# When a planned load that reuses a stored buffer counts as ready: landing instead of queue order

## The chip, the cores and the metric

The kernel runs on one core of one Trainium2 chip. The metric is the device time of one execution in microseconds (us); less is better. In the profile the engines are PE (TensorE), PEld (its weight loads), DVE (VectorE), ACT (ScalarE), POOL (GpSimd) and SP (SyncE). Here SP only issues DMA transfers, nearly all of them.

## What is computed

One layer of a streaming encoder in fp32 for 512 prompt tokens and 64 sample tokens, 576 in all, with D = 1024:

```python
mod = silu(c) @ w_ada + b_ada                    # six shift/scale/gate vectors of 1024
h = rms_normalize(x) * g_norm_mix * (1 + sc1) + sh1
q, k, v, qi, ki, wi, z, xbc, dt, gates = split(h @ w_in)
o_attn = dsa_attention(...)                      # indexer, top-k keys per query, softmax
y = ssd_scan(conv(xbc), dt, ...)                 # chunked scan, 8 groups; gated by silu(z), group norm
mixed = (sig(g1) * (o_attn @ w_branch_attn) + sig(g2) * (y @ w_branch_ssm)) @ w_out
x = x + gt1 * mixed
h2 = rms_normalize(x) * g_norm_ffn * (1 + sc2) + sh2
gate, up = split(h2 @ w_gate_up)                 # DFF = 2816
x = x + gt2 * ((silu(gate) * up) @ w_down)
```

It returns the new x, the new k, v and indexer keys, and the conv and scan states.

## The kernel before, in words

**Arithmetic.** Activations stand feature by token: 128 features on the partitions, and the 576 tokens as two halves of 288 (TH). Every fp32 operand is split into a rounded high part and the rest (wh and wl for weights, mh and ml, yh and yl and so on for activations), and a product is three matmuls: high by high, high by low, low by high. An output tile of 128 features, both halves, over 1024 inputs is 48 matmuls of 288 columns. A weight tile is loaded by SP into `raw` (two buffers), copied by ACT into `wh`, and subtracted by DVE into `wl`.

**Stages.** Modulation and norm at the start; w_in with the indexer, attention and 32 filler tiles (gates and z); conv and scan by groups g = 0 to 7; the branch projections; the output projection w_out with residual (`residual`, line 1681); the feed-forward, whose first two feature tiles are 16 plain products (twelve matmuls each) and the others seven products each of a Strassen scheme; w_down.

**The planner.** Nothing in the order of the instructions is written out by hand. `build` records every operation in a `Plan`. `_touch` (line 296) finds dependencies from the boxes of tiles that an operation reads and writes: `raw` (read after write), `waw`, and `war`, the latter also from the first writer of a buffer to all users of the tile that had the buffer before. A box is a bounding interval, on chip by partition and byte column, in a scratch tensor by offset. Two pieces with a stride, whose intervals interleave, thus count as overlapping even where they share no element.

`order` (line 402) then runs a list schedule over five engines with its own cost table (`cost`, line 347; `LATENCY`, line 233). `enable` is called for an operation once all its predecessors are placed; it works out the time t from which it is ready. Of the engine that is free first, the operation that is ready and has the smallest priority number (its place in the program, moved by `R.prio`) is placed. What the rules for t say is all the planner knows of waiting. For a DMA on SP, placed at time `at`, it reckons

```python
queue = max(at, queue) + 0.46
dma_free = max(queue + 1.3, dma_free) + op.xfer
op.t1 = dma_free + op.dur_dma
```

where t1 is the landing, `dur_dma` is 0.93, and `op.xfer` is the larger of bytes at `rate` (300e3 bytes per us after the start) and runs * (11.5 + 0.0358 * run bytes) / 16e3; SP itself is free again at once, or 2 us before `dma_free`. `emit` (line 573 issues everything, which is why each row of the profile has that line) hands the list to the tile framework in the planned order. Each engine executes its list in that order. The framework adds the semaphore waits that the buffers need, those of a load on the landing of an earlier store from the same buffer among them, whatever the planner assumed.

**Around the output projection.** `x2` are the tiles of the residual stream, tag `x2` with four buffers in pool `x1p`: `load_x2(a)` (line 1641) loads tile a from the scratch tensor x_d; `residual(a, ps, hf, last)` adds the projected tile to it, and behind the second half stores it and refills the buffer:

```python
if hf == 1:
    sync.dma_start(x2_d[:, a], x2[a])
    if 4 <= a + 3 < 8:
        load_x2(a + 3)
```

So `load_x2(4)` takes the buffer of x2[0], and so on to 7. The profile leaves buffer numbers out of names: both x_d and x2_d are `x_d` there, x2 is `x`, `x_d<-x` is the store of x2, `x<-x_d` the refill, and `x_d<-xs` the six stores of the input near the start (`store_x`, line 938).

In the same stage `ada_columns(7, ffw, 2, ("T3", "T4"), ("T1", "T2"))` (line 1699) works out one part of the modulation on DVE: eight pieces of w_ada of 256 KB go through the two tags T1 and T2, two buffers each (`T<-in_w_ada`), are multiplied and summed into T3 and T4, which sixteen small matmuls with `pick` bring together (`px<-T,pick`). `load_f(f)` (line 1784) loads the gate and up columns of feature tile f, tags `raw` and `rawu`, two buffers each; `prepare` (line 1802) splits them, for f = 1 partly into the tag `wx`. The last three tiles of w_out (a = 5, 6, 7) are done half by half, with accumulators in `mm` (two buffers, shared with the whole kernel) and `px`.

**Other places where a transfer follows a transfer in the same buffer.** `key_stack` (line 1157) loads a cache block twice into interleaved columns of one tile (`kisd`, `kd`, `kstd`). The narrow tile of w_in is loaded in two parts into one `raw`. The tiles g of the attention branch (four buffers) are loaded, gated, stored to m_d, and their buffers loaded again. The scratch tensors x_d, z_d, o_d, m_d and x2_d are written piece by piece with strides.

Of the kernel before, what the change touches and what calls it, by code (L numbers as in the profile page):

```python
# [229 lines left out]
class Plan:  # L230
# [171 lines left out]
    def order(self):  # L402
# [19 lines left out]
        def enable(op):  # L422
            closed = [p for p in op.pools if not p.open]
            if closed:
                held.setdefault(closed[0], []).append(op)
                return
            t = max((x[0].wait[x] for x in op.spots if x[0].kw.get("space") is None), default=0.0)
            for d, kind in op.deps.items():
                q = ops[d]
                if kind == "order" or q.mm and op.mm:  # L430
                    t = max(t, q.t0)
                elif kind == "raw" or q.eng != op.eng:
                    t = max(t, q.t1 + self.LATENCY[q.eng][op.eng] + op.slack)
            op.since = t
            heapq.heappush(future[op.eng], (t, op.prio, op.i))
# [25 lines left out]
        def fire():  # L461
            nonlocal now_ev
            while now_ev < len(self.events):
                what, p = self.events[now_ev]
                if what == "close" and p.ops_left:
                    return
                if p.kw.get("space") is None:
                    (place if what == "open" else leave)(p)
                seq.append((what, p))
                now_ev += 1  # L470
                if what == "open":
                    p.open = True
                    for op in held.pop(p, []):
                        enable(op)

        fire()
        for op in ops:
            if op.left == 0:
                enable(op)
        n = 0  # L480
        while n < len(ops):
# [16 lines left out]
            op = ops[i]  # L498
            if best == "tensor":
                if at - op.since < HOLD and self.change(form, op.form) > 0.1:  # L500
                    same = [x for x in r if ops[x[1]].form == form]
                    if same:
# [4 lines left out]
                        op = ops[x[1]]  # L507
                at += self.change(form, op.form)
                form = op.form
            if op.port:  # L510
                if port > at and best == "vector":
                    held_back = [(pr, i)]
                    while r and op.port and len(held_back) < 6:
                        pr, i = heapq.heappop(r)
                        held_back.append((pr, i))
                        op = ops[i]
                    pr, i = held_back.pop() if not op.port else held_back.pop(0)
                    op = ops[i]
# [22 lines left out]
            for s in op.succ:  # L541
                ops[s].left -= 1
                if ops[s].left == 0:
                    enable(ops[s])
# [1457 lines left out]
```

## Time and profile before

| | us |
|---|---|
| median of 3 runs | 1383.86 |
| lowest and highest | 1383.17 and 1384.22 |
| the profiled execution | 1383.03 |
| its span, first to last instruction | 1381.1 |
| busy in it: PE, DVE, ACT, POOL | 1356.7, 1071.9, 724.3, 209.8 |
| DMA, 190.19 MB, mean rate | 138 GB/s |

The profiled execution takes 1.9 us beyond its span. A busy PE isn't PE at its peak, since matmuls are pipelined and their ends modelled; what counts here are the gaps between them and the clock that was granted, which is 0.998 of full speed over the whole span. SP's rows are the instructions that issue transfers; their landing shows in the rows of what waits for them, and in the table of issues with the median time to landing.

### The profile page before, as it was taken

To read this page: it belongs to the slowest core of one execution; us is meant where nothing else is said; L and a number is where in the kernel's file an instruction comes from. 1 tells how busy PE (TensorE), PEld (TensorE's weight loads), DVE (VectorE), ACT (ScalarE), POOL (GpSimd) and SP (SyncE) were. 2 spreads that over 40 slices of the span, in tenths; PEclk is the share of its full clock that TensorE was granted. 3 is DMA by queue.
4 is the path that set the end of the run, shared out by engine and by line. 5 is a ranking of instruction groups with operands and counts; after the bars stand their busy time and mean duration, and the time that the engine had idled before them with its cause. 6 is when DMAs were issued, how large, how long until landed. Compare 5 with 4: busy or idle time off the path is not lost.

```text
span 1381.1 us, 27476 instructions
## 1 busy us (share of the span) xinstructions
PE 1356.7 (98%) x10731; PEld 1318.6 (95%) x10731; DVE 1071.9 (78%) x2115; ACT 724.3 (52%) x1542; POOL 209.8 (15%) x297
## 2 busy tenths in 40 slices
PE   7999999999999999999999999998999999999998
PEld 5999999999999999999999999998999999999998
DVE  5579997887878679888887688877899888887421
ACT  5444333767776655666665341224676666671221
POOL 2111003320300134444333300000000000000000
PEclk9999999999999999999999999999999999999999
DMA  9552347462753544344446477756233333326430
GB/s 324 164 132 83 113 121 205 115 164 69 194 135 88 129 120 118 110 125 133 121 118 189 135 217 228 251 180 205 72 92 93 92 94 103 95 87 215 141 110 29
DMA packets 252145, 190.19 MB, mean 138 GB/s; under 512 B 24768, under 2 KB 222640, under 8 KB 252016
## 3 DMA queue, kind: packets, MB, share of 16 engines
q1 hardware_dynamic: 248864, 177.87, 43.6%
q0 software_dynamic: 3104, 10.55, 4.1%
q8 instruction: 84, 1.38, 0.4%
q14 instruction: 45, 0.37, 0.1%
q10 hardware_dynamic: 48, 0.02, 0.0%
HBM read 153.09 MB, written 24.83 MB: 129 GB/s over the span
## 4 chain that ended last, share of the span: by engine, by line
PE 83%; DVE 9%; ACT 4%; DMA 2%; issue 1%; POOL 0%; SPq 0%; DVEq 0%; ACTq 0%; POOLq 0%
PE mm L573 61%; PE py L573 13%; PE px L573 9%; DVE cu L573 2%; DVE score L573 1%; DVE wl L573 1%; DVE m L573 1%; ACT wh L573 1%; DMA x_d<-x 1%; DMA T<-in_w_ada 1%; ACT dec L573 1%; DVE xb L573 1%; DMA rawu<-in_w_gate_up 0%; DMA rowsS<-in_c_sample 0%; DMA bc<-acs_d 0%
## 5 line engine op out<-in xcount | busy, mean ns | idle before, releaser
L573 ACT ACTIVATE wh<-raw 128x1024 fp32r<-128x1024 f32 (+1 forms) x159 | 156.4, 986 | 240.5 <-PE mm L573 193.1
L573 PE MATMUL mm<-hTl,wh 128*128 128x288 f32 x1152 | 262.5, 303 | 0.0
L573 PE MATMUL mm<-hTh,wl 128*128 128x288 f32 x1152 | 262.4, 303 | 0.0
L573 PE MATMUL mm<-hTh,wh 128*128 128x288 f32 x1152 | 259.9, 303 | 1.8 <-ACT hTh L573 1.8
L573 DVE TENSOR_TENSOR wl<-raw,wh 128x1024 fp32r<-128x1024 f32 (+1 forms) x117 | 142.2, 1217 | 86.4 <-ACT wh L573 81.8
L573 PEld LDWEIGHTS mm<-hTh,wl 128*128 128x128 f32 x1152 | 188.2, 189 | 2.8 <-issue 0.7
L573 PEld LDWEIGHTS mm<-hTh,wh 128*128 128x128 f32 x1152 | 186.2, 189 | 3.7 <-ACT hTh L573 2.1
L573 PEld LDWEIGHTS mm<-hTl,wh 128*128 128x128 f32 x1152 | 187.9, 189 | 1.6
L573 DVE SCALAR_TENSOR_TENSOR cu<-xc,wc,cu 128x579 f32<-128x579 f32 x96 | 90.3, 940 | 5.1 <-ACT cu L573 3.9
L573 PE MATMUL mm<-xhS,wh 128*128 128x290 f32 (+1 forms) x376 | 83.5, 296 | 0.0
L573 PE MATMUL mm<-xhS,wl 128*128 128x288 f32 (+1 forms) x360 | 80.0, 296 | 0.0
L573 DVE SCALAR_TENSOR_TENSOR aacc<-adr,sil,aacc 128x512 f32<-128x512 f32 x98 | 68.1, 744 | 6.6 <-DMA adr<-in_w_ada 6.6
L573 PE MATMUL mm<-wl,hTh 128*128 128x256 f32 x256 | 72.3, 284 | 0.1
L573 PE MATMUL mm<-wh,hTl 128*128 128x256 f32 x256 | 72.1, 284 | 0.0
L573 PE MATMUL mm<-wh,hTh 128*128 128x256 f32 x256 | 71.7, 283 | 0.0
L573 PE MATMUL mm<-xlS,wh 128*128 128x288 f32 (+1 forms) x252 | 65.9, 297 | 0.0
L573 PEld LDWEIGHTS mm<-xhS,wh 128*128 128x128 f32 x376 | 62.6, 188 | 0.0
L573 PEld LDWEIGHTS mm<-xhS,wl 128*128 128x128 f32 x360 | 60.0, 189 | 0.0
L573 PE MATMUL mm<-yl,wh 128*128 128x288 f32 x256 | 55.5, 297 | 0.0
L573 PE MATMUL mm<-yh,wl 128*128 128x288 f32 x256 | 55.0, 296 | 0.0
L573 PE MATMUL mm<-yh,wh 128*128 128x288 f32 x256 | 54.8, 296 | 0.0
L573 ACT ACTIVATE P<-lg,mn 128x128 f32<-128x128 f32 (+4 forms) x72 | 41.8, 581 | 24.8 <-DVE mn L573 23.9
(462 smaller groups left out, 3596.8 us busy)
## 6 DMA issues: line engine op xcount, KB each, us to landing
raw<-in_w_in SPq DMA_DIRECT2D x80, 512.0 KB, 4.0
adr<-in_w_ada SPq DMA_DIRECT2D x44, 512.0 KB, 5.7
rawu<-in_w_gate_up SPq DMA_DIRECT2D x22, 512.0 KB, 3.9
raw<-in_w_gate_up SPq DMA_DIRECT2D x22, 512.0 KB, 3.8
wl<-raw POOLq DMA_DIRECT2D x20, 512.0 KB, 4.8
bc<-acs_d SPq DMA_DIRECT2D x32, 256.0 KB, 3.4
raw<-in_w_branch_ssm SPq DMA_DIRECT2D x16, 512.0 KB, 4.6
raw<-in_w_down SPq DMA_DIRECT2D x16, 512.0 KB, 4.3
```

Source lines behind the costliest of these rows:

```text
L573: getattr(engines[x.eng], x.fn)(*[real(a) for a in x.args], **{k: real(v) for k, v in x.kw.items()})
```

## The change

One condition in `enable`, in the loop over the predecessors `d` of an operation (`q` is the predecessor, t1 its end and for a transfer its landing, t0 its start):

```diff
                 if kind == "order" or q.mm and op.mm:
                     t = max(t, q.t0)
-                elif kind == "raw" or q.eng != op.eng:
+                elif kind == "raw" or q.eng != op.eng or q.fn == "dma_start":
                     t = max(t, q.t1 + self.LATENCY[q.eng][op.eng] + op.slack)
```

Before, a `war` or `waw` predecessor on the operation's own engine put no bound on t. After, it puts t behind the landing, where that predecessor is a transfer. No operation, buffer, priority or cost is changed. What changes is the list that the planner makes, from the first place on where such a pair alters a choice.

## The prediction

> **What bounds the kernel now.** I read the page first, for the engine that sets the time.
>
> ```profile
> PE 1356.7 (98%) x10731; PEld 1318.6 (95%) x10731; DVE 1071.9 (78%) x2115; ACT 724.3 (52%) x1542; POOL 209.8 (15%) x297
> ```
>
> TensorE is busy in all but 1381.1 - 1356.7 = 24.4 us of the span. The change adds and removes no instruction; it only reorders queues. So it can win no more than part of those 24.4 us, and what counts is where they lie. The table of stretches says (after the stretch: its length, then busy time of PE, PEld, DVE, ACT and POOL; then granted clock, DMA share, GB/s):
>
> ```profile
> 800.00:920.00 120.00, 120.00 (x945) 118.19 (x944) 101.22 (x157) 33.49 (x48) 0.44 (x4) 1.00 0.72 224
> 920.00:960.00 40.00, 36.25 (x284) 34.74 (x283) 29.61 (x62) 17.72 (x40) 0.50 (x2) 0.98 0.66 200
> 960.00:1000.00 40.00, 39.96 (x297) 39.73 (x296) 30.02 (x57) 21.95 (x47) 2.01 (x4) 0.98 0.33 101
> 1000.00:1230.00 230.00, 230.00 (x1717) 229.84 (x1716) 203.11 (x356) 154.28 (x301) 0.00 (x0) 1.00 0.31 90
> ```
>
> Between 800 and 1230 us TensorE stops only in one place, 920:960, where the output projection hands over to the feed-forward part. It loses 3.75 us there. The timeline of TensorE shows the gaps (in brackets, idle before and what ended it):
>
> ```profile
> 952.72 0.29 PE L573 MATMUL px<-mh,wh 128*128 128x288 f32 x1
> 953.85 0.43 PE L573 MATMUL px<-T,pick 128*32 128x128 f32 x8 [0.85 <-DVE T L573]
> 954.52 0.43 PE L573 MATMUL px<-T,pick 128*32 128x128 f32 x8 [0.24 <-DVE T L573]
> ...
> 956.59 0.40 PE L573 MATMUL px<-mh,wl 128*128 128x288 f32 x1 [1.32 <-DVE wl L573]
> ...
> 958.47 0.61 PE L573 MATMUL mm<-mh,wh 128*128 128x288 f32 x1 [1.35 <-DVE x L573]
> ```
>
> 0.85 + 0.24 + 1.32 + 1.35 = 3.76 us, each time VectorE being late. The chain of waits says why VectorE is late (start, duration, what):
>
> ```profile
> 942.30 6.90 DMA x_d<-x
> ...
> 950.16 5.75 DMA rawu<-in_w_gate_up
> ```
>
> The path runs through the landing of a store of x2 (the profile drops buffer numbers: here x is a tile x2, x_d is x2_d), and then through a weight load queued behind it. SyncE's waits have the sum (us, times, longest), and its timeline the places:
>
> ```profile
> SPq L573 <- DMA x_d<-x: 15.6, 4, 5.4
> ```
>
> ```profile
> 925.13 0.34 SPq L573 DMA_DIRECT2D x_d<-x  x1
> ...
> 927.32 0.33 SPq L573 DMA_DIRECT2D x<-x_d  x1
> ...
> 933.43 0.33 SPq L573 DMA_DIRECT2D x_d<-x  x1
> 939.00 0.33 SPq L573 DMA_DIRECT2D x<-x_d  x1
> 939.44 1.66 SPq L573 DMA_DIRECT2D T<-in_w_ada  x2
> ...
> 942.30 2.55 SPq L573 DMA_DIRECT2D x_d<-x  x1
> 949.25 0.34 SPq L573 DMA_DIRECT2D x<-x_d  x1
> 949.64 0.42 SPq L573 DMA_DIRECT2D T<-in_w_ada  x1
> 950.16 0.38 SPq L573 DMA_DIRECT2D rawu<-in_w_gate_up  x1
> 950.63 0.53 SPq L573 DMA_DIRECT2D x_d<-x  x1
> 956.65 0.33 SPq L573 DMA_DIRECT2D x<-x_d  x1
> ```
>
> Four times a store of x2 is followed by the load that refills its buffer; SyncE stands at the load until the store has landed (from issue to the next load: 2.2, 5.6, 6.95 and 6.0 us), and the loads of T and rawu stand behind it. The planner of before believes such a load is ready at once, because store and load share a queue.
>
> **The change part by part.** The planner now holds a same-queue successor of a transfer until the transfer's modelled landing. For a store of x2 (294,912 B in runs of 2,304 B) its own formulas give 0.46 + 1.30 + 0.98 + 0.93 + 0.10 = 3.77 us. That is no time of the chip, only the length of the hold. During it SyncE takes other ready transfers. By the buffer rules these pairs are hit:
>
> (a) *The four refills of x2.* The third is worth the most. SyncE finished issuing the store at 942.30 + 2.55 = 944.85; T and rawu, now at 949.64 and 950.16, can go out at about 944.9 and 945.4, 4.7 us earlier. What they release:
>
> ```profile
> 953.05 1.42 DVE L573 SCALAR_TENSOR_TENSOR T<-T,sil,T 128x512 f32<-128x512 f32 x2 [3.64 <-DMA T<-in_w_ada]
> 954.38 1.03 DVE L573 SCALAR_TENSOR_TENSOR x<-mm,gt1h,x 128x256 f32<-128x256 f32 x3
> 955.32 1.22 DVE L573 TENSOR_TENSOR wl<-raw,wh 128x1024 fp32r<-128x1024 f32 x1
> 956.59 1.29 DVE L573 TENSOR_TENSOR wx<-rawu,wx 128x512 fp32r<-128x512 f32 x2
> ...
> 966.10 0.64 DVE L573 SCALAR_TENSOR_TENSOR x<-px,gt1h,x 128x256 f32<-128x256 f32 x2 [0.92 <-PE px L573]
> ```
>
> ```profile
> 955.93 1.15 ACT L573 ACTIVATE wx<-rawu 128x512 fp32r<-128x512 f32 x2 [5.42 <-DMA rawu<-in_w_gate_up]
> ```
>
> VectorE was free 3.64 us before 953.05, so its pair on T starts at 949.4; wl, right behind, ends at 956.54 - 3.64 = 952.9. TensorE, which leaves its last unhindered matmul at 952.85, then meets T and wl on time: 0.85, 0.24 and 1.32 us go. The last wait hangs on rawu: landing at 955.91 - 4.7 = 951.2, ScalarE then splits it, VectorE does wx from 952.95, and the x that frees the accumulator comes as long after wx as now (958.47 - 956.59 = 1.88), at 954.83. TensorE would be there at 958.47 - 3.76 = 954.71. So 0.12 us remains at best. The other bound: the chip's landings (up to 6.0 us at the fourth pair) exceed the hold of 3.77, so SyncE can still stand 6.0 - 3.77 = 2.2 us at an earlier refill, and T and rawu gain only 2.5 us. T's pair then starts at 950.55, wl ends at 954.05, x comes at 954.1 + 1.88 = 955.98, and 1.27 us remains. I take the middle, 0.7: the landings before it, 2.2 and 5.6 us, lie on both sides of the hold. The other three stalls pay nothing of their own: TensorE has no gap behind the first two, since VectorE's work for it came early enough, and none from 960 on behind the fourth.
>
> (b) *TensorE's clock behind the stall.* The stretches of TensorE alone (busy, granted clock, DMA share, GB/s):
>
> ```profile
> 958.40:961.50 3.10, 3.03 (x12) 0.50 1.10 321
> ```
>
> ```profile
> 961.51 0.30 PE L573 MATMUL mm<-mh,wh 128*128 128x288 f32 x1
> ...
> 963.12 0.29 PE L573 MATMUL px<-ml,wh 128*128 128x288 f32 x1
> ```
>
> After the gaps it runs at half clock for 3 us: twelve matmuls take 961.51 - 958.47 = 3.04 us, the next twelve 963.12 - 961.51 = 1.61. That is 1.43 us lost, and it goes if the stall goes. Whether a rest of 0.7 us would still trip it, no row shows; the shortest single gap with a half-clock stretch behind it is this, 1.83 us:
>
> ```profile
> 742.14 0.81 PE L573 MATMUL mm<-hTh,wh 128*128 128x288 f32 x4 [1.83 <-ACT hTh L573]
> ```
>
> I take it as gone, since 0.7 is well under 1.83. (The Trainium skill, "TensorE: Matmul & The Clock Gate", Part 1: the clock falls to half after at least one idle window of about 3.4 us, windows running freely, and returns after a busy one. The return agrees with the 3 us here; the fall doesn't, since 1.83 us sufficed. By its 3.4 us a rest of 1.27 us would be harmless too, and the sum at that end would stay 3.92 us rather than 2.49.)
>
> (c) *The refills themselves* go out later in the queue. The tightest is the fourth: issued at 956.65, read by VectorE at 966.10. Loads of its kind take 5.8 us:
>
> ```profile
> x<-x_d SPq DMA_DIRECT2D x8, 288.0 KB, 5.8
> ```
>
> It lands at 962.45 now. Its store can go once the third stall is gone, about 2.7 us earlier; with the hold it is issued near 951.7 and lands near 957.5, while the reader moves to 966.10 - 4.5 = 961.6. Cost 0, with 4 us of cover; without it, up to the hold.
>
> (d) *Pairs elsewhere.* Writes to neighbouring strided pieces of one tile or scratch tensor count as overlapping, so the planner also holds the second of the two cache loads of each key stack, the second part of the narrow w_in tile, and each of the stores into x_d, z_d, m_d, x2_d behind the one before. Their readers are far off; the first key stack stands for them:
>
> ```profile
> L573 PE MATMUL px<-ident,kisd x9: 270/272/316, 78.4 to 81.5; 128*128 128x128 f32 x9
> L573 SPq DMA_DIRECT2D kisd<-in_cache_ki x2: 379/442/505, 46.0 to 46.4; - x2
> ```
>
> 46.4 against 78.4 leaves 32 us for a hold under 4. The six stores of x into x_d, near the start, are read only in the output projection, and the last x2_d stores gate the pools of the feed-forward evacuation, whose first accumulators are wanted again only after the sixteen plain products. Direct cost 0. What they can do is displace a neighbour in the queue, and shift every later choice of the planner a little; with no row for it I bound it by the 1.83 us gap above, either way, and take 0.
>
> **Sum.** 3.76 - 0.7 + 1.43 = 4.5 us. Behind 960 us TensorE is the bound (230.00 busy of 230.00), so the gain reaches the end. The profiled execution took 1383.03 us (span 1381.1 and 1.9 around it), 0.83 below the median of the runs: 1383.03 - 4.5 = 1378.5 for it, 1383.86 - 4.5 = 1379.4 for the median. The case's own range is 3.92 to 5.07: 1378.8 to 1379.9.
>
> **The rivals.** A difference of 0.2%, 2.8 us, is about what a measurement of this kernel tells from none.
>
> *Shifted stall.* The hold of 3.77 is shorter than the landings of 5.6 to 6.95. If the planner sees nothing else ready, the load is still picked too early, and SyncE stands there for the rest. At the worst end of (a) with the clock still dropping, the gain is 3.76 - 1.27 = 2.49 us: 1381.4. For it: three of four landings are longer than the hold. Against: T and rawu are ready behind the load and pass it in the hold.
>
> *Nothing happens.* The other transfers are not ready in the plan's time, the order stays, 1383.9. Against: rawu's second buffer has had no user yet, and T's was released in the trace before 944.9, with the last use of the piece whose buffer it takes:
>
> ```profile
> 939.78 0.74 DVE L573 SCALAR_TENSOR_TENSOR T<-T,sil,T 128x512 f32<-128x512 f32 x1
> ```
>
>
> *Slower, by a displaced load in the scan stage.* The gap at 742.14 comes from the same cause elsewhere:
>
> ```profile
> 730.75 5.14 DMA bc<-acs_d
> ```
>
> A small load of bc, issued late by SyncE, holds GpSimd, ScalarE and then TensorE, for 1.83 us and a half-clock stretch of about 1.43: 3.26 us. The scan has eight groups with such loads; if the shifted plan puts bc behind a weight load that waits for its buffer, each case costs as much. It decides when three new ones arise (9.8 - 4.5 = +5.3: 1389.2), or one with the gain above lost (1387.1). For it: SyncE's queue is in order and the planner's times drift. Against: the only pairs of the change in that stage are stores and refills of g that follow whole output tiles of 48 matmuls each, at 1.61 / 12 = 0.13 us some 6.4 us apart, longer than the hold. The reverse, that gap healed too, gives 1379.4 - 3.26 = 1376.1.
>
> **How the numbers follow.** Forecast 0.46, shifted stall 0.20 (half of it beyond 2.8 us), nothing or a gain cancelled by a small loss 0.17, slower 0.13, more than forecast 0.04. Faster 0.46 + 0.04 + 0.10 = 0.60; same 0.17 + 0.10 = 0.27; slower 0.13. The likeliest gives 1379.4. The range goes down by the 1.83 us of drift from the best end, 1378.8 - 1.8 = 1377.0, and up to one new stall with the worst of the shifted gain: 1381.4 + 3.26, some 1384.7, and by the 0.83 us between runs to 1385.5; beyond it lies most of the slower case, below 1377.0 the case of more than forecast.
>
> **What would show it.** Right: SyncE's wait on x2's stores falls from 15.6 to under 8 us; T and rawu stand ahead of the third refill; TensorE's busy time in the stretch rises to over 39 of 40 with its clock at 1.00. Wrong: the 15.6 stays; or it falls and VectorE's waits for T and rawu don't; or the gaps move to another stage, the scan above all.

## The result and the profile after

| | us |
|---|---|
| before, median of 6 runs (lowest to highest) | 1383.69 (1383.17 to 1384.35) |
| after, median of 6 runs (lowest to highest) | 1375.03 (1374.49 to 1376.97) |
| ratio, with its 95% interval | 0.9939 (0.9927 to 0.9952) |
| profiled execution after, and its span | 1376.16, 1374.5 |

The change makes the kernel 8.7 us faster by the medians, 0.6%. The forecast was 4.5 us (1379.4), and its range ended at 1377.0. The mechanism that the forecast named is there, but a second gain stands beside it that the forecast had taken as zero. The rest of the text separates the two.

The page of the kernel after, its busy times and the first line of its chain of waits:

```profile
PE 1355.4 (99%) x10731; PEld 1318.0 (96%) x10731; DVE 1070.2 (78%) x2115; ACT 722.4 (53%) x1542; POOL 212.0 (15%) x297
...
PE 86%; DVE 8%; ACT 3%; issue 1%; DMA 1%; POOL 0%; DVEq 0%; ACTq 0%; POOLq 0%
```

TensorE's idle time falls from 24.4 us to 1374.5 - 1355.4 = 19.1 us. The table of stretches of the kernel after, with the columns that the prediction used:

```profile
910.00:960.00 50.00, 50.00 (x395) 48.92 (x395) 39.85 (x78) 20.80 (x48) 0.81 (x4) 1.00 0.71 218
960.00:1000.00 40.00, 39.96 (x302) 39.72 (x301) 34.72 (x61) 25.00 (x52) 1.70 (x2) 1.00 0.21 65
1000.00:1230.00 230.00, 230.00 (x1717) 229.86 (x1716) 203.19 (x357) 156.00 (x301) 0.00 (x0) 1.00 0.32 94
```

The stall of 3.75 us at 920 to 960 is gone entirely, and the clock stands at 1.00 on both sides of 960. SyncE's waits in the stretch 905 to 985 and its timeline show why:

```profile
SPq L573 <- DMA x_d<-x: 3.7, 1, 3.7
```

```profile
932.15 0.47 SPq L573 DMA_DIRECT2D x_d<-x  x1
933.84 2.98 SPq L573 DMA_DIRECT2D T<-in_w_ada  x3
936.87 0.43 SPq L573 DMA_DIRECT2D rawu<-in_w_gate_up  x1
938.02 0.38 SPq L573 DMA_DIRECT2D raw<-in_w_out  x1
938.73 2.33 SPq L573 DMA_DIRECT2D x_d<-x  x1
941.16 0.38 SPq L573 DMA_DIRECT2D x<-x_d  x1
941.59 0.44 SPq L573 DMA_DIRECT2D rawu<-in_w_gate_up  x1
944.49 0.38 SPq L573 DMA_DIRECT2D raw<-in_w_gate_up  x1
945.41 0.34 SPq L573 DMA_DIRECT2D x_d<-x  x1
945.85 4.44 SPq L573 DMA_DIRECT2D x<-x_d  x2
```

Of 15.6 us of standing, 3.7 are left. Between the second store (`x_d<-x`, 932.15) and the refill that needs its buffer (`x<-x_d`, 941.16) there are now loads of T, rawu and raw. The last pieces of T go out by 936.8, and the second rawu at 941.59. Before, they went at 949.64 and 950.16, behind the third refill. VectorE in the same stretch:

```profile
945.30 1.41 DVE L573 SCALAR_TENSOR_TENSOR T<-T,sil,T 128x512 f32<-128x512 f32 x2
947.00 0.74 DVE L573 SCALAR_TENSOR_TENSOR T<-T,sil,T 128x512 f32<-128x512 f32 x1
...
950.17 1.22 DVE L573 TENSOR_TENSOR wl<-raw,wh 128x1024 fp32r<-128x1024 f32 x1
```

The idle time of 3.64 us before the pair on T has gone, and wl begins at 950.17 where it began at 955.32.

For the rest of the program, the stretches of TensorE alone (length, busy, clock, DMA share, GB/s), before and then after:

```profile
60.00:470.00 410.00, 407.15 (x3067) 1.00 0.51 129
470.00:520.00 50.00, 49.34 (x405) 1.00 0.40 110
...
725.00:760.00 35.00, 33.17 (x260) 0.95 0.66 191
...
900.00:970.00 70.00, 66.25 (x516) 0.98 0.61 182
```

```profile
60.00:470.00 410.00, 407.93 (x3081) 1.00 0.51 130
470.00:520.00 50.00, 50.00 (x414) 1.00 0.42 110
...
725.00:760.00 35.00, 33.17 (x267) 0.95 0.66 196
...
900.00:970.00 70.00, 70.00 (x558) 1.00 0.63 192
```

Beside the 3.75 us at 900 to 970 there are 0.78 us at 60 to 470 and 0.66 us at 470 to 520, long before the first refill. The gap of the scan stage, at 725 to 760, is neither healed nor made worse.

### The profile page after: what moved, and what is told of

Read it like the earlier page. It is cut to its first block, busy times and chain, and to the rows that moved or that the text cites. A ratio compares the mean times of both kernels' runs of the same rounds, so it can differ in the third digit from the quotient of the medians.

```text
span 1374.5 us, 27487 instructions
## 1 busy us (share of the span) xinstructions
PE 1355.4 (99%) x10731; PEld 1318.0 (96%) x10731; DVE 1070.2 (78%) x2115; ACT 722.4 (53%) x1542; POOL 212.0 (15%) x297
## 4 chain that ended last, share of the span: by engine, by line
PE 86%; DVE 8%; ACT 3%; issue 1%; DMA 1%; POOL 0%; DVEq 0%; ACTq 0%; POOLq 0%
PE mm L573 64%; PE py L573 13%; PE px L573 9%; DVE cu L573 1%; DVE score L573 1%; DVE wl L573 1%; DVE m L573 1%; ACT wh L573 1%; DVE xb L573 0%; ACT dec L573 0%; DMA rowsS<-in_c_sample 0%; DMA raw<-in_w_in 0%; DMA bc<-acs_d 0%; ACT xc L573 0%; DVE qst L573 0%
## 5 line engine op out<-in xcount | busy, mean ns | idle before, releaser
L573 ACT ACTIVATE dec<-dec,nacs 128x128 f32<-128x128 f32 x128 | 41.6, 393 | 24.0 <-POOL dec L573 23.3
```

The lines of the kernel that those rows point to most:

```text
L573: getattr(engines[x.eng], x.fn)(*[real(a) for a in x.args], **{k: real(v) for k, v in x.kw.items()})
```

## The experiments

Set side by side, the instruction lists of before and after differ for TensorE in two stretches only: from the start to about 480 us, and around 920 to 960. Between about 500 and 900 us they are the same. Hence the theories that the expectations name. **A**: the gain comes from two places, the refills of x2 and the early list, and the two add up. **B**: all of it comes from the refills, and the early differences are worth nothing. Then, for the early part: **C**: a small shift anywhere near the start sets the planner on another course, and that course happens to be better; the pairs themselves cost nothing. **D**: the early pairs held real waits on the chip, which the change heals.

Most edits narrow or bend the new condition in `enable`; all are made on the kernel before, if nothing else is said. The kernel before ran beside them again: its median is 1383.45 for experiments 1 to 3, 1383.15 for 4, 8 and 9, and 1383.52 for 5 to 7. The difference of the medians and the ratio can put a gain up to some 1 us apart; where that matters both are given.

**1. The refills of x2 alone.**

```diff
-                elif kind == "raw" or q.eng != op.eng:
+                elif kind == "raw" or q.eng != op.eng or q.fn == "dma_start" and op.fn == "dma_start" and getattr(op.args[0].base, "tag", None) == "x2":
```

> Only the refills of x2 are held until the store has landed; up to the first refill the list is the old one word for word. Theory A (two places: the stage around 920-960 gives its whole stall and half-clock stretch, 3.75 + 1.43 = 5.2 us, and the rest of the 8.7 comes from other pairs): 1383.7 - 5.2 = 1378.5 us, between 1377.7 and 1379.3, TensorE busy 40 of 40 in 920-960, everything before 920 us as before the change. Theory B (all of it comes from the refills): 1375.0, between 1374.3 and 1376.5.

Measured: 1377.97 us (1377.7 to 1379.05, 5 runs) against 1383.45 (27 runs of before); ratio 0.9964 (0.995 to 0.9978), that is -5.5 us by the medians and -5.0 by the ratio. TensorE by stretches:

```profile
470.00:520.00 50.00, 49.34 (x406) 1.00 0.40 108
...
900.00:970.00 70.00, 70.00 (x559) 1.00 0.64 195
```

The stall and its half-clock stretch are gone as after the whole change, and the early 0.66 us of idle time stands as before. So the refills give some three fifths of the gain, and B falls.

**2. Everything but the refills.**

```diff
+                elif kind == "raw" or q.eng != op.eng or q.fn == "dma_start" and not (op.fn == "dma_start" and getattr(op.args[0].base, "tag", None) == "x2"):
```

> All other same-queue pairs are held, the refills of x2 are not. Theory A: the rest, 8.7 - 5.2 = 3.5 us, so 1380.2, between 1379.3 and 1381.5, with the stall of 3.75 us at 920-960 still there and about 1.1 us of idle less before 740 us. Theory B: 1383.7, within 0.8.

Measured: 1380.76 (1379.3 to 1382.61, 11 runs); ratio 0.9985 (0.9976 to 0.9994), -2.7 us by the medians and -2.1 by the ratio, whose interval is -3.3 to -0.8.

```profile
60.00:470.00 410.00, 407.98 (x3081) 1.00 0.50 130
470.00:520.00 50.00, 50.00 (x413) 1.00 0.40 110
...
725.00:760.00 35.00, 32.83 (x294) 1.00 0.68 203
...
900.00:970.00 70.00, 66.91 (x519) 0.98 0.60 179
```

The mirror image: the early stretches are those of after, the stall at 900 to 970 stays (3.09 us in this execution). By the medians -5.5 and -2.7 add to -8.2, next to -8.7 for the whole; by the ratios -5.0 and -2.1 add to -7.1, next to -8.4, which the intervals allow. A holds: there are two gains, and within the noise they add.

**3. Parts of the early pairs.** Once the caches (`kisd`, `kd0`, `kstd`), once the narrow w_in tile and the stores of x into x_d:

```diff
+ ... or q.fn == "dma_start" and op.fn == "dma_start" and getattr(op.args[0].base, "tag", "") in ("kisd", "kd0", "kstd"):
```

> Only the second cache load of each key stack is held. Theory A leaves open which early pair gives the rest; if the attention stage does, 1382 or less with TensorE's 0.66 us idle at 470-520 gone; if the start does, 1383.7 within 0.8. Theory B: 1383.7.

Measured: 1380.77 (1379.24 to 1382.98, 11 runs); ratio 0.9984 (0.9975 to 0.9992), -2.7 us by the medians and -2.2 by the ratio.

```diff
+ ... or q.fn == "dma_start" and op.fn == "dma_start" and (getattr(op.args[0].base, "tag", None) == "raw" or q.i < op.i < 900 and op.args[0].base.pool is None):
```

> Only the second part of the narrow w_in tile and the chain of the six stores of x into x_d are held. Theory A: this and the cache loads together give the 3.5 us; if the start gives it, 1380 to 1382 here. Theory B: 1383.7 within 0.8.

Measured: 1379.62 (1378.13 to 1382.48, 11 runs); ratio 0.9978 (0.9969 to 0.9986), -3.8 us by the medians and -3.0 by the ratio, a little more than the expectation's 1380 to 1382.

These two touch different pairs, and each gives all of the early gain; together, in experiment 2, they give no more than one. Their lists join that of after, the one from about 100 us on, the other from about 200. That speaks for C: what pays is the course on which the planner ends up, not the pair that sent it there.

**4. One early pair at a time.** First only `kstd`, then, with the other name in the same line, only `kisd`, the first key stack of the indexer (one load of 128 KB is held):

```diff
+ ... or q.fn == "dma_start" and op.fn == "dma_start" and getattr(op.args[0].base, "tag", "") == "kstd":
```

> Only the second cache loads of the last three key stacks are held; no engine's list but SyncE's changes, and there only by a few places between 200 and 400 us. Theory C (the early gain is another course of the whole list, not anything that the held transfers do themselves): the time as before the change, within 0.8 us. Theory D (holding the cache loads helps, by less contention or by freeing SyncE): a part of the 2.7 us, 1382.5 or less.

Measured: 1383.75 (1381.02 to 1385.17, 11 runs) against 1383.15; ratio 1.0 (0.9991 to 1.0009).

> Only one load of 128 KB is held, the second of the indexer's key stack at 46 us, read at 78 us. It sends the planner onto the other course: from 100 us to 480 us TensorE's list is that of the change, before it and behind it that of before. Theory C: the whole early gain from this one harmless transfer, 2.7 us within 1.0, TensorE's 0.66 us idle at 470-520 gone. Theory D: no more than a fifth of it, 0.5 us.

Measured: 1380.98 (1378.52 to 1383.06, 11 runs); ratio 0.998 (0.9972 to 0.9989), -2.2 us by the medians, -2.8 by the ratio.

With `kstd` only SyncE's list changes, by a few places, and the lists of the other engines stay: no gain. With `kisd` alone the list joins that of after at about 100 us, and the whole early gain is there. The load that it holds is read 32 us later, as the prediction showed, and SyncE's waits of the kernel before have no entry for a transfer of these tiles. So there was no wait of SyncE to heal, and for this pair D falls. For the pairs of the second edit of experiment 3 D has no such test. SyncE's waits on `raw<-in_w_in` are 7.0 us before and 5.4 there, but also 6.8 in experiment 2 and 9.7 with `kisd` alone, which have the gain as well.

**5. Shifting the planner in another way.** The slack that it adds to every dependency, 0.25 us, is set a hundredth up or down, and the rule is left as before:

```diff
-SLACK = 0.25
+SLACK = 0.26
```

> The old rule; only the planner's slack in front of TensorE goes from 0.25 to 0.26, a change with no reason in the chip that reshuffles the list from the start on. Theory C (the gain outside the output projection is the luck of a reshuffled list): the idle time before 740 us moves by up to 1.5 us either way, the time by up to 3 us, no sign favoured: 1380.5 to 1386.5. Theory D (holding the early pairs heals real waits there): such a reshuffle gives nothing, 1383.5 within 0.8.

> As the one with 0.26, in the other direction: slack 0.24. Theory C: 1380.5 to 1386.5, and not the same as with 0.26; theory D: 1383.5 within 0.8.

Measured: with 0.26, 1382.83 (1381.33 to 1384.02, 10 runs) against 1383.52, ratio 0.9993 (0.9984 to 1.0002); with 0.24, 1381.79 (1378.95 to 1384.64, 10 runs), ratio 0.9986 (0.9977 to 0.9995). SyncE's waits with 0.26:

```profile
SPq L573 <- DMA x_d<-x: 15.6, 4, 5.5
```

The refills stand about as long as before (14.1 us with 0.24), so these two kernels show what a mere shift of the list is worth: nothing that can be told from none, and -1.7 us. The early gain of the change, -2.7 us, is of that size, if somewhat more. None of the three lists is slower than before; three draws are too few to say whether a sign is favoured.

**6. The refill freed in another way.** If the gain at 920 to 960 comes from SyncE no longer standing at the refill, a fifth buffer must bring it as well, with the planner's rule left alone. The load is held to the end of the residual step, so that it doesn't come earlier than it did:

```diff
-        x2[a] = x1p.tile([P, 2, TH], F32, name=f"x2{a}", tag="x2", bufs=4)
+        x2[a] = x1p.tile([P, 2, TH], F32, name=f"x2{a}", tag="x2", bufs=5)
...
-            vec.scalar_tensor_tensor(x[:, c0:c0 + n], ...
+            done = vec.scalar_tensor_tensor(x[:, c0:c0 + n], ...
...
+                R.after = [done]
                 load_x2(a + 3)
+                R.after = ()
```

> The old rule everywhere, but x2 has five buffers instead of four and each refill is ordered behind the addition of its own step, so that no refill follows a store into the same buffer closely: the wait is taken away by a buffer, not by the rule. If SyncE's standing at the refills is what cost the stage (theory A): SyncE's wait on x2's stores 0, TensorE 40 of 40 in 920-960, 1378.0, between 1377.2 and 1379.0, as with the rule for x2 alone. If the rule helped by something else, such as another order of the weight splits: 1381 or more.

Measured: 1378.22 (1377.54 to 1379.29, 5 runs) against 1383.52; ratio 0.996 (0.9948 to 0.9973), -5.3 us. The waits of SyncE have no entry for `x_d<-x` any more, and TensorE by stretches:

```profile
725.00:760.00 35.00, 32.81 (x267) 1.00 0.68 197
...
900.00:970.00 70.00, 70.00 (x561) 1.00 0.64 197
```

The same gain as in experiment 1 (-5.5), by another edit. That shows the cause: what cost 5.3 to 5.5 us was a load at the head of the queue whose buffer was still being stored, with two needed loads behind it. The buffer did not do it alone, though. The refills also stand later in this list; the first went out at 927.32 before, and here it reads

```profile
930.33 0.38 SPq L573 DMA_DIRECT2D rawu<-in_w_gate_up  x1
932.16 0.38 SPq L573 DMA_DIRECT2D raw<-in_w_out  x1
932.70 1.45 SPq L573 DMA_DIRECT2D x_d<-x  x1
934.21 0.42 SPq L573 DMA_DIRECT2D x<-x_d  x1
```

What a fifth buffer gives with the refill in its old place was not tried.

**7. A longer hold.** The refills of x2 alone, held for 2.5 us more than the modelled landing:

```diff
+ ... getattr(op.args[0].base, "tag", None) == "x2":
+                    late = 2.5 if q.fn == "dma_start" and q.eng == op.eng and kind == "war" else 0.0
+                    t = max(t, q.t1 + self.LATENCY[q.eng][op.eng] + op.slack + late)
```

> The rule for the refills of x2 alone, with their hold lengthened by 2.5 us, to about the landings that the chip shows (6 us). Theory A says the remaining wait of SyncE (3.7 us once) is covered: SyncE's wait on x2's stores 0 to 1 us, the time unchanged, 1378.0 within 0.8. The rival, that the rest of the stall's cost is still in the time: 1376.5 or less. If the later refills come too late for their readers: 1380 or more, with VectorE waiting on them.

Measured: 1378.92 (1378.9 to 1379.22, 5 runs); ratio 0.9965 (0.9953 to 0.9978). SyncE's wait for the stores is gone from the list altogether, and yet there is no further gain: 0.9 us more than experiment 1 by the medians, just outside the 0.8 that was expected, with overlapping intervals of the ratio. The hold has begun to cost VectorE something, which now waits for the last refill:

```profile
962.11 0.64 DVE L574 SCALAR_TENSOR_TENSOR x<-px,gt1h,x 128x256 f32<-128x256 f32 x2 [2.16 <-DMA x<-x_d]
```

TensorE has no gap at 900 to 970 (70.00 of 70.00), but one behind it that experiment 1 has not:

```profile
972.49 0.40 PE L574 MATMUL mm<-xhA,wh 128*128 128x290 f32 x1 [0.52 <-ACT wh L574]
```

Experiment 6, whose refills are late as well, has the same gap of 0.52 us; whether the refills cause it isn't shown.

So the modelled landing is long enough, although the stores land later than the model says, and the 3.7 us for which SyncE still stands after the change lie beside work that nobody is late for.

**8. The gap of the scan.** It is still there after the change:

```profile
741.07 0.87 PE L573 MATMUL mm<-hTh,wh 128*128 128x288 f32 x4 [1.82 <-ACT hTh L573]
```

On the kernel after, the tile bc gets a third buffer, so that its load can go earlier:

```diff
-        bc = sd.tile([P, 4, P], F32, name=nm + "bc", tag="bc", bufs=2)
+        bc = sd.tile([P, 4, P], F32, name=nm + "bc", tag="bc", bufs=3)
```

> The change, and three buffers for bc in the scan instead of two, so that the load whose lateness makes TensorE rest 1.8 us at 741 need not wait for GpSimd. If it heals that gap and its half-clock stretch: 1.8 us, and up to 1.4 more in the executions that had the stretch, so 1372 to 1373.3. Since the list from 450 us on is reshuffled by it, theory C allows up to 1.5 us either way on top: 1371 to 1375. If the gap is not from bc: 1375 within 1.5, with ScalarE still late at that place.

Measured: 1375.29 (1375.24 to 1376.99, 5 runs) against 1383.15; ratio 0.9942 (0.993 to 0.9955). The gap and the stretches of TensorE:

```profile
743.20 0.54 PE L573 MATMUL mm<-hTh,wh 128*128 128x288 f32 x2 [0.58 <-DVE sg L573]
```

```profile
470.00:520.00 50.00, 48.95 (x398) 1.00 0.43 113
...
725.00:760.00 35.00, 34.42 (x295) 1.00 0.65 208
760.00:900.00 140.00, 139.28 (x1137) 1.00 0.65 205
```

The gap shrinks from 1.82 to 0.58 us, and 725 to 760 gains 34.42 - 33.17 = 1.25 us of work. But the list has been shuffled again: 50.00 - 48.95 = 1.05 us are lost at 470 to 520 and 140.00 - 139.28 = 0.72 at 760 to 900, so nothing is left. The time lies 0.3 us above the range that was expected for a healed gap.

**9. The change once more**, beside experiment 8:

> The change itself once more, beside the others on one chip: 1375.0, between 1374.3 and 1377.0. The stretch at half clock behind the gap at 741 comes in some executions and not in others, so the times should spread over about 1.5 to 2.5 us, with a granted clock of 0.998 in the long ones and 1.000 in the short ones.

Measured: 1376.36 (1374.82 to 1376.8, 5 runs); ratio 0.9942 (0.9929 to 0.9956), -6.8 us by the medians and -8.0 by the ratio, where the first measurement gave -8.7 and -8.4. The runs spread over 2 us as expected, the three above 1376 with a clock of 0.998 and the two below with 0.999. The ratio is that of experiment 8. No version here is shown to be faster than the change.

## Why the prediction was wrong, point by point

**(a) The refills: right in kind, and better than its middle.** T and rawu went ahead of the third refill as described, SyncE's wait fell to 3.7 us (under 8 was asked for), and the chain T, wl, wx, x moved forward. The prediction left a rest of 0.7 us (0.12 to 1.27) because T and rawu would gain only 2.5 to 4.7 us. They gained more, since loads of T and rawu now pass the first and second refill too: the last T stands at 933.84 to 936.82 and rawu at 941.59, 8 us and more ahead of their old places (about 1 us of it is the earlier list, whose first store goes at 924.03 instead of 925.13). The rest is 0: TensorE has 70.00 of 70.00 at 900 to 970.

**(b) The half-clock stretch: right.** Granted clock 1.00 where 0.98 stood. 3.75 us of idle time and about 1.4 of half clock make 5.2. Measured alone, the refills gave 5.5 and 5.3 by the medians (5.0 and 5.5 by the ratios), with intervals wide enough for 5.2. The best end of the forecast's own case was 5.07. The 3.75 is itself one draw: in the eight profiled executions with the old order there, TensorE's idle time at 900 to 970 lies between 2.70 and 3.91 us. The reason that the prediction gave, a rest of 0.7 well under 1.83, was not put to the test, since no rest stayed; behind the gaps of 0.52 and 0.58 us in experiments 7 and 8 the clock stands at 1.00.

**(c) The later refills: right.** No cost shows. The 4 us of cover aren't measured: in experiment 7, with 2.5 us more of hold, VectorE waits 2.16 us for the last refill, but the list around it has changed as well.

**(d) Pairs elsewhere: this step failed.** "... with no row for it I bound it by the 1.83 us gap above, either way, and take 0." No direct cost shows: with `kstd` held alone the time stays. But the drift of the planner, put at nothing in the sum, measures -2.7 us by the medians and -2.1 by the ratio (experiment 2). That is clear of zero; it is beyond the bound by the medians, while the interval of -3.3 to -0.8 includes the bound. This term decides: without it the result would be 1383.7 - 5.5 = 1378.2, inside the range. With it, and with only the forecast 4.5 from the refills, the time would be 1376.7 by the medians and 1377.3 by the ratio, at the range's end of 1377.0; the rest of 0.7 us that part (a) expected and that didn't come takes it further out. The mistake was to take 0 and to bound it as narrowly as that. The 1.83 us were one gap in one stage, while the drift touches the whole list from the start to 480 us, in which TensorE of before stood idle for 9.56 us in the first 60 us, 2.85 in the next 410, and 0.66 at 470 to 520. Part of these was open to a better list. No row of the trace gave its sign; experiment 5 shows that two other shifts give -0.7 (not clear of zero) and -1.7, so with hindsight some 2 to 3 us would have been the fair bound.

**The rivals.** The shifted stall did not come as a cost: the other loads were ready within the hold, and the one wait of 3.7 us that SyncE keeps is not felt by TensorE. The slower case did not come either: the gap of the scan neither multiplied nor went. "More than forecast" (0.04) was right about the time, which fell below the range, but named the wrong place, that gap.

**Open.** Of the 2.7 us of the early list (2.1 by the ratio) the profile shows 1.56 as idle time of TensorE before 725 us: 14.14 us before (9.56 + 2.85 + 0.66 + 1.07), 12.58 in experiment 2 (9.50 + 2.02 + 0 + 1.06). Some 0.2 us lie outside the span: time less span is 1.93 us on average in the 27 runs of before and 1.72 in the 11 of experiment 2. The rest, 0.3 to 0.9 us, isn't located, and one profiled execution of each can't locate it. That of before has the half-clock stretch in the scan and that of experiment 2 has not, and the stall at 900 to 970 is 3.75 us in the one and 3.09 in the other, with the same list there. Why the second edit of experiment 3 is 1.1 us below the first isn't settled either; their intervals overlap. C's word "happens" is supported by experiments 3 to 5 and not proved: it is shown that no single pair is the cause, not that every list of that kind is better by luck.

## What to carry to other kernels

Look in SyncE's timeline for a load at the head of the queue that waits for a store from its own buffer, and read what stands behind it: the cost is the lateness of those loads at the engine that sets the time, here some 5 us, where SyncE stood for 15.6. A later place in the list takes it away, by the planner's rule (experiment 1) or together with an extra buffer (experiment 6). Where a planner orders the whole program, any edit to its rules also moves everything else: give that drift a bound of its own, from the idle time in the part that the edit can reshuffle, and measure it by undoing the intended part alone. A gain of that sort belongs to this one list, and the next edit may give it back, as the third buffer of bc did at 470 to 520 us.

## What the runs showed of the hardware that was not expected

**The same gap halves the clock in some executions and not in others.** In the profiled execution of before, the 1.83 us in the scan are followed by this (TensorE alone, with the clock before the DMA share):

```profile
742.20:745.30 3.10, 3.10 (x16) 0.64 0.61 182
```

In experiment 2, where the gap is 1.81 us and ends at 740.46, the stretch as close behind it reads

```profile
740.52:743.62 3.10, 3.10 (x24) 1.00 0.64 192
```

with 24 matmuls started instead of 16. In thirteen of the fourteen profiled executions (all but experiment 8) the gap lies between 1.66 and 1.83 us. The clock at 725 to 760 is 0.95 in six of them (before, after twice, experiment 1, the first of 3, `kisd` of 4) and 1.00 in seven (experiments 2, 6 and 7, the second of 3, `kstd` of 4 and the two of 5). By the 1.43 us that the prediction read behind the other stall, one such stretch costs about 1.4 us, which is 0.001 of 1380 us and so 0.001 of the mean clock. The spread of the runs goes the same way, though a mean doesn't say where the clock fell: of 69 runs of before, three had a mean clock of 0.996 (mean time 1384.49), 46 of 0.997 (1383.61), 13 of 0.998 (1383.28), seven of 0.999 (1381.91). The Trainium skill, "TensorE: Matmul & The Clock Gate", Part 1, has the clock fall after at least one idle window of about 3.4 us, with windows that run freely. That the outcome varies for one and the same gap fits windows that run freely; the length doesn't fit, since 1.81 to 1.83 us sufficed where it happened.

**Equal stores land after very different times.** The four stores of x2 in the kernel before, all of 288 KB on one queue, lie between 2.2 and 6.95 us ahead of the load that waits for them, where the planner reckons 3.77 for each. The third of them contains 2.55 us in which SyncE was still issuing. What else makes the difference was not tried. It was enough, all the same, to place the refill by the fixed figure.
